# Projection of the last recurrent channel block before, instead of after, the MLP of the compressed values

## The chip, the cores and the metric

The kernel runs on one core of one Trainium2 chip. TensorE (PE) multiplies matrices into PSUM, VectorE (DVE) and ScalarE (ACT) read PSUM and work elementwise, GpSimd (POOL) works elementwise in SBUF, and the queue of SyncE (SP) issues nearly all DMAs. Each engine takes its own instructions in their order and waits on semaphores for the others. The metric is the device time of one execution in microseconds (us), the median of several runs.

## The reference, cut to what matters

One decoder block on x of shape (1024 tokens, 1024 channels). After an RMS norm one projection feeds two mixers, whose results are gated, added and projected out:

```
proj = rms_norm(x) @ w_in
y_a  = nsa_mixer(...)            # 8 heads in 2 groups: compressed, selected, sliding-window attention
y_b  = rglru_mixer(u_lru, ...)   # 512 channels
x + (sigmoid(gate_a) * (y_a * silu(g_nsa)) @ w_proj_a
     + sigmoid(gate_b) * (y_b * silu(g_lru)) @ w_proj_b) @ w_out
```

Two parts of it matter here. The recurrent mixer: a causal convolution of width 4 over `u`, two gates `r` and `i` from small block matrices, and a scan `h = a*h + b` over the 1024 tokens, with `a = exp(-8 r softplus(-lambda))`. And the compression of keys and of values: blocks of 32 tokens are flattened, 2048 inputs to 256 hidden units with SiLU, then 64 outputs, `silu(flat @ w1 + b1) @ w2`, once for keys (`kc`) and once for values (`vc`).

## The kernel before

All products of float32 values are made from a high and a low part: `mm3` (lines 170 to 173) issues three matmuls, high by high (L171), low by high (L172, the low part of the activations) and high by low (L173). A weight is loaded into `w_raw` (L177, two buffers), its high part is made by ACT (`w_hi`, L185, two buffers) and the low part by POOL or DVE (`w_lo`, L186). `hT_h` and `hT_l` (tiles `big_h`, `big_l`) hold the normed input, transposed.

After the norm the program has a stretch in which three kinds of work lie side by side on PE.

- `lru(n)` for the four channel blocks n of 128 channels. Its first part (call it A) projects `u` and the gate input: two chunks of 48 matmuls of 512 columns, then the copy to SBUF (L344), the convolution on DVE (L349, three times L352), the split (L355, L356) and a SiLU (L362, L363). Its second part (B) has four groups of three gate matmuls into `ps_t` (two buffers), each read by ACT as a sigmoid (L371); then ACT L377, L378 and L379 with table loads between them, DVE L380, L381, L383, L382 and the scan L384, POOL L372 and L385, and the store of the result to `yb` (L386).
- `compress()`: first the projections of keys and values, then for each of the two (j = 0 keys, j = 1 values) the copies of the blocks, the loads of w1 in eight pieces (L416, into buffers of `ph`, `pl` and `ev`), the MLP's first layer on PE (L422, 32 products in pairs of instructions), ACT L432, DVE L433 and L434, the second layer (L439) and, for the values, the split into `vcc` (L462, L463). The eighth piece of w1 goes into an `ev` buffer that the second piece has left, so its load is issued when the second piece's products are done.
- `qkv(0)`: queries, keys and values of the first head group, eight tiles of 128 tokens, 48 matmuls of 262 columns each; two of its four weight pieces are split into the tile `p_slc`, which compress() used before. Each tile's result is copied by ACT into an `ev` buffer (L519, L520; three buffers) and prepared by `prep`: ACT L552, DVE L554, POOL L193 and L194, DVE L557, POOL L558 and L559, ACT L562, L566 and L570, DVE L563 and L567, POOL L571, PE transposes L575 and L582 into `ps_t`, and their copies L577 and L586.

Queries, keys and the recurrent blocks' temporaries share nine tiles `t`. After this stretch comes the attention, in which the second group's projections and the merge's projections fill PE between the attention's own matmuls.

The order in which the pieces are written is set by a string; `0` to `3` stand for the next part of a recurrent block and `c` for the next part of `compress()`:

```
parts = {"0": lru(0), "1": lru(1), "2": lru(2), "3": lru(3), "c": compress()}
for k in ORD:
    next(parts[k])
```

With `ORD = "0c1c0c2c1c323"` the end reads: B of block 1, the MLP of the values, A of block 3, B of block 2, B of block 3. The framework's scheduler then puts the instructions of each engine into an order of its own by priorities (roughly the written order) and its own idea of when each could start, so a change of the string moves instructions on every engine for some way on.

Of the kernel before, what the change touches and what calls it, by code (L numbers as in the profile page):

```python
# [41 lines left out]
RW = 1  # L42
LE = 1
IE = 0
ORD = "0c1c0c2c1c323"
YE = 0
JE = 15
UE = 15
# [39 lines left out]
def _build(ctx, tc, A, out, dbg):  # L88
# [378 lines left out]
# [3 lines that stand above are left out]
# [662 lines left out]
```

## Time and profile before

| what | us |
|---|---|
| median of 3 runs (lowest, highest) | 893.48 (892.17, 894.21) |
| the profiled execution | 894.25 |
| its span, first to last instruction | 892.50 |
| PE busy in the span | 868.9 (97%) |
| DVE, ACT, POOL busy | 539.1, 449.8, 298.3 |

A row of the timeline gives the start, the length, the engine, line, operation, tile written <- tiles read, the shapes and the count, and in brackets how long the engine had been idle and what released it. A PE matmul's length is modelled to its end in the pipeline; the next matmul starts earlier, so starts are compared with starts. In a row of windows the busy time of each engine is followed by the number of its instructions, and the last three numbers are the granted clock of TensorE (1.00 is 2.4 GHz, 0.50 is 1.2 GHz), the busy share of the DMA engines and the GB/s.

### The profile page before, as it was taken

The page shows a single profiled execution, that of the slowest core. Times are in us where ns is not written, and L with a number is a line of the kernel's source. Part 1 is how long each engine was busy: PE and PEld are TensorE (multiplying, and loading weights), DVE is VectorE, ACT ScalarE, POOL GpSimd, SP SyncE. Part 2 cuts the span into 40 slices and gives each one's busy share as a digit, 9 for nine tenths or more (in the row PEclk, how much of TensorE's full clock was granted, in tenths as well). Part 3 has the DMA queues.
Part 4 walks back from the last instruction along what each step waited for, and adds up shares of the span by engine and source line. Part 5 has one row for each costly group of instructions (what it writes and reads, how often), then busy time and mean ns, then how long its engine had stood idle before and what let it go on. Part 6 is the DMA issues. An engine that isn't in the chain of part 4 may idle for free.

```text
span 892.5 us, 15853 instructions
## 1 busy us (share of the span) xinstructions
PE 868.9 (97%) x5670; PEld 778.3 (87%) x5670; DVE 539.1 (60%) x1629; ACT 449.8 (50%) x1168; POOL 298.3 (33%) x338
## 2 busy tenths in 40 slices
PE   5999999989999999999999999999999899999998
PEld 4778888889999999999999998999999887888887
DVE  4564547586423547566677857667777878892111
ACT  7322645845524647566556757566666563440000
POOL 4032243297512526244256644233334432000000
PEclk9999999999999999999999999999999999999999
DMA  9134420121312112211112241111114379971111
GB/s 352 58 98 117 158 84 26 63 71 51 131 45 84 59 67 72 66 60 65 53 62 77 75 140 53 33 70 55 33 45 127 128 245 341 362 257 71 71 72 47
DMA packets 45519, 92.49 MB, mean 104 GB/s; under 512 B 6896, under 2 KB 12704, under 8 KB 45440
## 3 DMA queue, kind: packets, MB, share of 16 engines
q1 hardware_dynamic: 44480, 88.33, 29.5%
q0 software_dynamic: 960, 3.15, 0.9%
q8 instruction: 44, 0.72, 0.3%
q14 instruction: 35, 0.29, 0.1%
HBM read 64.15 MB, written 25.21 MB: 100 GB/s over the span
## 4 chain that ended last, share of the span: by engine, by line
PE 82%; POOL 5%; ACT 4%; DMA 3%; DVE 3%; issue 1%; SPq 0%; POOLq 0%; ACTq 0%; DVEq 0%
PE ps_f L171 10%; PE ps_f L172 10%; PE ps_f L173 10%; PE ps_s L633 7%; PE ps_s L171 6%; PE ps_s L173 6%; PE ps_s L172 6%; PE ps_t L686 6%; PE ps_t L171 3%; PE ps_t L172 3%; PE ps_t L173 3%; PE ps_o L711 3%; PE ps_o L710 3%; DMA w_raw<-in_w_out 1%; PE ps_s L422 1%
## 5 line engine op out<-in xcount | busy, mean ns | idle before, releaser
L172 PE MATMUL ps_f<-big_l,w_hi 128*128 128x256 f32 (+1 forms) x712 | 204.8, 288 | 0.0
L171 PE MATMUL ps_f<-big_h,w_hi 128*128 128x256 f32 (+1 forms) x664 | 193.7, 292 | 1.0 <-ACT ev L852 0.9
L173 PE MATMUL ps_f<-big_h,w_lo 128*128 128x256 f32 (+1 forms) x664 | 189.3, 285 | 0.0
L172 PEld LDWEIGHTS ps_f<-big_l,w_hi 128*128 128x128 f32 x712 | 135.0, 190 | 2.3
L171 PEld LDWEIGHTS ps_f<-big_h,w_hi 128*128 128x128 f32 x664 | 125.2, 189 | 5.0 <-ACT ev L852 2.5
L173 PEld LDWEIGHTS ps_f<-big_h,w_lo 128*128 128x128 f32 x664 | 124.8, 188 | 1.8 <-POOL w_lo L186 0.3
L691 DVE TENSOR_TENSOR pl<-ps_t,ph 128x512 fp32r<-128x512 f32 x132 | 90.4, 687 | 47.1 <-ACT ph L690 45.7
L186 POOL TENSOR_TENSOR w_lo<-w_raw,w_hi 128x1024 fp32r<-128x1024 f32 x32 | 77.4, 2422 | 97.7 <-ACT w_hi L185 75.7
L690 ACT ACTIVATE ph<-ps_t 128x512 fp32r<-128x512 f32 x132 | 78.2, 600 | 49.5 <-PE ps_t L686 45.3
L671 POOL TENSOR_SCALAR p_slc<-p_slc,mx,bg 128x384 f32<-128x384 f32 (+7 forms) x88 | 68.6, 785 | 87.3 <-DVE mx L670 33.1
L667 ACT ACTIVATE p_slc<-ps_s,mx 128x256 f32<-128x256 f32 (+5 forms) x128 | 68.2, 541 | 23.4 <-DVE mx L665 16.6
L172 PE MATMUL ps_s<-big_l,w_hi 128*128 128x512 f32 x172 | 69.6, 405 | 0.0
L185 ACT ACTIVATE w_hi<-w_raw 128x1024 fp32r<-128x1024 f32 (+1 forms) x40 | 42.4, 1062 | 42.8 <-PE ps_f L172 17.3
L657 DVE TENSOR_REDUCE mx<-ps_s 128x1 f32<-128x256 f32 (+5 forms) x120 | 51.0, 437 | 10.5 <-PE ps_s L633 9.2
L710 PE MATMUL ps_o<-ph,t 128*128 128x512 f32 x132 | 55.5, 420 | 0.0
L171 PE MATMUL ps_s<-big_h,w_hi 128*128 128x512 f32 x136 | 54.1, 406 | 0.3 <-ACT big_h L246 0.3
L686 PE MATMUL ps_t<-ident_r,p_slc 128*128 128x128 f32 x336 | 54.0, 273 | 0.0
L173 PE MATMUL ps_s<-big_h,w_lo 128*128 128x512 f32 x136 | 54.0, 399 | 0.0
L662 DVE CUSTOM_DVE_ANT_0 ps_s<-ps_s,bias 128x256 f32<-128x256 f32 (+1 forms) x128 | 52.6, 417 | 1.6 <-PE ps_s L633 0.5
L633 PE MATMUL ps_s<-kTs,t 128*128 128x512 f32 (+4 forms) x224 | 52.9, 348 | 0.5 <-ACT pc L642 0.3
L711 PE MATMUL ps_o<-pl,t 128*128 128x512 f32 x132 | 53.2, 403 | 0.0
L671 POOL TENSOR_SCALAR p_win<-p_win,mx,bg 128x640 f32<-128x640 f32 (+1 forms) x40 | 35.0, 878 | 49.7 <-DVE mx L670 22.2
(368 smaller groups left out, 2182.2 us busy)
## 6 DMA issues: line engine op xcount, KB each, us to landing
w_raw<-in_w_in SPq DMA_DIRECT2D x30, 512.0 KB
t<-in_x SPq DMA_DIRECT2D x8, 512.0 KB
gb<-ev SPq DMA_DIRECT2D x16, 256.0 KB
ga<-ev SPq DMA_DIRECT2D x16, 256.0 KB
w_raw<-in_w_out SPq DMA_DIRECT2D x8, 512.0 KB
st<-mb SPq DMA_DIRECT2D x16, 256.0 KB
w_raw<-in_w_tok SPq DMA_DIRECT2D x6, 524.0 KB
ev<-in_cw SPq DMA_DIRECT2D x8, 256.0 KB
```

Of the source, the lines that this page charges most:

```text
L171: T.matmul(o, lh, rh, start=first, stop=False)
L172: T.matmul(o, lh, rl, start=False, stop=False)
L173: T.matmul(o, ll, rh, start=False, stop=last)
L186: (E or (V if tail else G)).tensor_tensor(out=lo, in0=raw, in1=f(hi), op=OP.subtract)
L633: T.matmul(s, qT[h][:, i * 128:(i + 1) * 128], rhs, start=(hl == 0), stop=(hl == 1))
L667: C.activation(p[:, h, k0:k1], sv, AF.Exp, bias=mx[:, 6:7], accum_out=mx[:, 7 + j:8 + j])
L671: G.tensor_scalar(out=p[:, h], in0=p[:, h], scalar1=mx[:, 9:10], scalar2=bg[:, g, i, 4 * (br + 1) + h:4 * (br + 1) + h + 1], op0=OP.mult, ...
L686: ins = T.transpose(pt[:, h * 128:(h + 1) * 128], p[h][:, c0:c0 + 128], ident)
L690: C.activation(ph, pt, AF.Copy)
L691: V.tensor_tensor(out=pl, in0=pt, in1=f(ph), op=OP.subtract)
L710: T.matmul(o, vf, pp[0], start=first, stop=False)
L711: T.matmul(o, vf, pp[1], start=False, stop=False)
```

## The change

One letter of the order string changes places with its neighbour: A of block 3 is written ahead of the MLP of the values.

```diff
-ORD = "0c1c0c2c1c323"
+ORD = "0c1c0c2c13c23"
```

No operation is added or removed. What the scheduler makes of it differs on every engine, from the last gates of block 1 to the first units of the attention; from there on the orders are the same again. On PE the 32 products of L422 move behind the 96 chunk matmuls of block 3 and stand there in one piece, directly ahead of qkv(0). Three places are shown.

On SP's queue, around the loads of the token weights (`w_raw<-in_w_tok`) and the eighth piece of w1 (`ev<-in_cw`), the difference is:

```order
 L498 DMA p_win<-in_w_tok 128x1048 x2
 L386 DMA yb<-t 128x1024
-L177 DMA w_raw<-in_w_tok 128x1048
+L177 DMA w_raw<-in_w_tok 128x1048 x3
+L386 DMA yb<-t 128x1024
 L416 DMA ev<-in_cw 128x512
 L177 DMA w_raw<-in_w_tok 128x1048
 L426 DMA t<-in_cw 128x128
-L386 DMA yb<-t 128x1024
-L177 DMA w_raw<-in_w_tok 128x1048 x2
```

The store of block 1's result (the second `yb` row) now stands ahead of the eighth piece of w1 and not behind it, and two more loads of token weights stand ahead of that piece.

On POOL, at the first tiles of `prep` (`ss_1355`, `sq_1353`, `ev_1349` belong to the first tile, `1446`, `1444`, `1440` to the second, `1537`, `1535`, `1531` to the third; `t_1203` is block 2's result), the order before was:

```order
L193 TENSOR_SCALAR ss_1355<-ss_1355 128x6
L194 TENSOR_TENSOR ss_1355<-ss_1355,nhalf_77 128x6
L385 TENSOR_TENSOR t_1203<-t_1203,kTs_427 128x1024
L558 TENSOR_TENSOR sq_1353<-sq_1353,small_73 128x256
L559 TENSOR_TENSOR sq_1353<-sq_1353,small_73 128x128
L571 TENSOR_TENSOR t_1271<-ev_1349,t_1271 128x64
L571 TENSOR_TENSOR t_1271<-ev_1440,t_1271 128x64
L571 TENSOR_TENSOR t_1272<-ev_1349,t_1272 128x64
L571 TENSOR_TENSOR t_1272<-ev_1440,t_1272 128x64
L193 TENSOR_SCALAR ss_1446<-ss_1446 128x6
```

and it is now, from block 2's L385 on:

```order
L385 TENSOR_TENSOR t_1203<-t_1203,kTs_427 128x1024
L558 TENSOR_TENSOR sq_1444<-sq_1444,small_73 128x256
L559 TENSOR_TENSOR sq_1444<-sq_1444,small_73 128x128
L193 TENSOR_SCALAR ss_1537<-ss_1537 128x6
L571 TENSOR_TENSOR t_1271<-ev_1349,t_1271 128x64
L571 TENSOR_TENSOR t_1271<-ev_1440,t_1271 128x64
L571 TENSOR_TENSOR t_1271<-ev_1531,t_1271 128x64
L194 TENSOR_TENSOR ss_1537<-ss_1537,nhalf_77 128x6
L571 TENSOR_TENSOR t_1272<-ev_1349,t_1272 128x64
```

The last reader of the first tile's `ev_1349` was the third L571 behind block 2's L385, straight after the first tile's own products; it now stands behind those of the second tile, the root L194 of the third and three more L571. The fourth tile's eviction (L519 into `ev_1622`) uses that buffer again.

On DVE the last block's chain (`t_1236`, `t_1235` belong to block 3) stood before in this order, from its first operation to its scan:

```order
L380 SCALAR_TENSOR_TENSOR t_1236<-t_1108,t_1236 128x1024
L381 SCALAR_TENSOR_TENSOR t_1235<-t_1108,t_1235 128x1024
L476 COPY bias_1247<-t_1248 128x1024
L554 TENSOR_REDUCE ss_1446<-sq_1444 128x6
L563 TENSOR_TENSOR st_1376<-sq_1353,st_1376 128x4x64
L383 TENSOR_TENSOR t_1176<-t_1176,t_1236 128x1024
L567 TENSOR_TENSOR st_1379<-sq_1353,st_1379 128x2x128
L476 COPY bias_1247<-t_1251 128x1024
L382 TENSOR_SCALAR t_1235<-t_1235 128x1024
L521 COPY bg_358<-ps_f_1451 128x12
L481 COPY cbias_357<-t_1254 128x512
L557 TENSOR_TENSOR sq_1444<-ev_1440,ss_1446 128x384
```

(one L554 and the scan L384 follow), and now the second tile's L557 stands ahead of it and the third tile's inside it:

```order
L557 TENSOR_TENSOR sq_1444<-ev_1440,ss_1446 128x384
L554 TENSOR_REDUCE ss_1537<-sq_1535 128x6
L380 SCALAR_TENSOR_TENSOR t_1236<-t_1051,t_1236 128x1024
L381 SCALAR_TENSOR_TENSOR t_1235<-t_1051,t_1235 128x1024
L476 COPY bias_1247<-t_1248 128x1024
L563 TENSOR_TENSOR st_1467<-sq_1444,st_1467 128x4x64
L567 TENSOR_TENSOR st_1470<-sq_1444,st_1470 128x2x128
L383 TENSOR_TENSOR t_1119<-t_1119,t_1236 128x1024
L476 COPY bias_1247<-t_1251 128x1024
L382 TENSOR_SCALAR t_1235<-t_1235 128x1024
L557 TENSOR_TENSOR sq_1535<-ev_1531,ss_1537 128x384
```

Behind these follow L577, L521, L554, L481 and the scan L384. Block 3's operations have fallen back by one tile of `prep`.

## Rows read from the trace of the kernel before

**Rows 1.** The page's head: span, and busy time of TensorE.

```profile
span 892.5 us, 15853 instructions
PE 868.9 (97%) x5670; PEld 778.3 (87%) x5670; DVE 539.1 (60%) x1629; ACT 449.8 (50%) x1168; POOL 298.3 (33%) x338
```

**Rows 2.** Windows of 5 us: length, then busy us of PE, PEld, DVE, ACT, POOL, then granted clock, DMA share, GB/s.

```profile
170.00:175.00 5.00, 3.27 (x26) 3.02 (x26) 2.40 (x3) 4.96 (x6) 0.00 (x0) 1.00 0.00 0
...
185.00:190.00 5.00, 3.21 (x28) 3.00 (x26) 5.00 (x8) 1.99 (x8) 4.76 (x6) 1.00 0.46 141
...
195.00:200.00 5.00, 3.12 (x27) 2.91 (x26) 4.22 (x8) 2.25 (x8) 4.83 (x5) 1.00 0.02 7
```

**Rows 3.** Timeline of PE: the four late starts between 170 and 205 us, and the matmul ahead of the second.

```profile
174.62 0.50 PE L171 MATMUL ps_t<-t,bias 128*128 128x512 f32 x1 [1.73 <-ACT t L371]
...
187.69 0.28 PE L173 MATMUL ps_s<-p_slc,big_l 128*128 128x262 f32 x1
189.76 0.54 PE L575 MATMUL ps_t<-ident_r,st 128*128 128x128 f32 x4 [1.79 <-DVE st L563]
...
199.12 0.54 PE L575 MATMUL ps_t<-ident_r,st 128*128 128x128 f32 x4 [1.89 <-DVE t L577]
...
203.73 0.54 PE L582 MATMUL ps_t<-ident_r,st 128*128 128x128 f32 x4 [0.24 <-DVE t L586]
```

**Rows 4.** Timeline of PE: the first and the fourth product of L422 for the values, the first and the 43rd of a run of chunk matmuls without a break, the first of a run of 262 columns, and the last matmul of the last gate group.

```profile
126.65 0.38 PE L422 MATMUL ps_s<-p_slc,ph 128*128 128x128 f32 x2
...
127.32 0.39 PE L422 MATMUL ps_f<-p_slc,ph 128*128 128x128 f32 x2
...
148.96 0.50 PE L173 MATMUL ps_s<-big_h,w_lo 128*128 128x512 f32 x1
...
158.78 0.40 PE L173 MATMUL ps_s<-big_h,w_lo 128*128 128x512 f32 x1
...
176.13 0.40 PE L173 MATMUL ps_t<-t,bias 128*128 128x512 f32 x1
...
178.31 0.28 PE L171 MATMUL ps_s<-w_hi,big_h 128*128 128x262 f32 x1
```

**Rows 5.** Timeline of SP's queue: the eighth piece of w1, the store of block 1, and two token weights behind it (256, 512 and 524 KB, the row of two loads is the span from the first to the second).

```profile
129.33 0.33 SPq L416 DMA_DIRECT2D ev<-in_cw  x1
...
154.04 0.33 SPq L386 DMA_DIRECT2D yb<-t  x1
154.47 8.30 SPq L177 DMA_DIRECT2D w_raw<-in_w_tok  x2
```

**Rows 6.** Windows of 2 us around the store: the last two numbers are the DMA share and GB/s.

```profile
154.00:156.00 2.00, 2.00 (x10) 1.62 (x9) 1.97 (x4) 0.87 (x2) 0.02 (x1) 1.00 0.60 229
156.00:158.00 2.00, 2.00 (x10) 1.65 (x9) 1.93 (x3) 0.00 (x0) 0.00 (x0) 1.00 0.92 293
```

**Rows 7.** Timeline of ACT: block 1's L379; then block 3's last two sigmoids, its L377 and its L379.

```profile
138.88 1.06 ACT L379 ACTIVATE t<-t 128x1024 f32<-128x1024 f32 x1
...
176.15 1.25 ACT L371 ACTIVATE t<-ps_t,small 128x512 f32<-128x512 f32 x2
177.44 1.15 ACT L377 ACTIVATE t<-t,m4sp 128x1024 f32<-128x1024 f32 x1
...
182.91 1.06 ACT L379 ACTIVATE t<-t 128x1024 f32<-128x1024 f32 x1
```

**Rows 8.** Timeline of DVE: block 1's L382 and block 3's; a tile's L557 beside POOL's L385 and one alone; block 3's L380 and its scan.

```profile
145.07 2.95 DVE L382 TENSOR_SCALAR t<-t 128x1024 f32<-128x1024 f32 x1
...
182.41 2.75 DVE L557 TENSOR_TENSOR sq<-ev,ss 128x384 f32<-128x384 f32 x1 [1.17 <-POOL ss L194]
...
185.16 1.21 DVE L380 SCALAR_TENSOR_TENSOR t<-t 128x1024 f32<-128x1024 f32 x1
...
191.96 0.80 DVE L382 TENSOR_SCALAR t<-t 128x1024 f32<-128x1024 f32 x1
...
195.04 2.58 DVE L384 TENSOR_TENSOR_SCAN t<-t 128x1024 f32<-128x1024 f32 x1
...
210.05 0.56 DVE L557 TENSOR_TENSOR sq<-ev,ss 128x384 f32<-128x384 f32 x1 [1.01 <-POOL ss L194]
```

**Rows 9.** Timeline of POOL: block 1's L385, L194 of the first tile (beside a scan on DVE) and of a later one, block 3's L385.

```profile
150.70 3.32 POOL L385 TENSOR_TENSOR t<-t,kTs 128x1024 f32<-128x1024 f32 x1 [3.24 <-DVE t L384]
...
179.06 3.31 POOL L194 TENSOR_TENSOR ss<-ss,nhalf 128x6 f32<-128x6 f32 x1
...
198.29 1.32 POOL L194 TENSOR_TENSOR ss<-ss,nhalf 128x6 f32<-128x6 f32 x1
199.58 2.39 POOL L385 TENSOR_TENSOR t<-t,kTs 128x1024 f32<-128x1024 f32 x1
```

**Rows 10.** Windows of 1 us around another late start of PE, with the granted clock as the third number from the end.

```profile
692.00:693.00 1.00, 0.00 (x0) 0.00 (x0) 1.00 (x1) 1.00 (x4) 1.00 (x2) 1.00 0.00 0
...
694.00:695.00 1.00, 1.00 (x5) 1.00 (x6) 1.00 (x4) 0.66 (x3) 0.86 (x1) 0.51 0.73 176
...
697.00:698.00 1.00, 1.00 (x9) 1.00 (x8) 0.97 (x2) 0.00 (x0) 0.00 (x0) 0.78 0.89 289
```

**Rows 11.** Timeline of PE: that start.

```profile
693.95 0.54 PE L171 MATMUL ps_f<-big_l,w_hi 128*128 128x256 f32 x1 [1.97 <-DVE ev L899]
```

## The prediction

> **What bounds the kernel now.** First the page's head: PE is busy 868.9 of 892.5 us [rows 1], so only PE's late starts and its share of other engines' waits can be won or lost. Then the windows: of the stretch that the change touches, three windows of 5 us show PE at 3.27, 3.21 and 3.12 us [rows 2]. The timeline of PE names the causes: at 174.62 it waits for a gate sigmoid on ACT (the buffers of `ps_t` are both in use), at 189.76 for the first tile's split on DVE (L563), at 199.12 and 203.73 for copies out of `ps_t` (L577, L586) that stand behind block 3's scan on DVE or its L385 on POOL [rows 3]. A PE row is modelled 0.28 us long, but the next 262-column matmul starts (187.69 - 178.31) / 77 = 0.122 us later [rows 3, 4], so each late start lost 0.16 us more than its idle time. The four lost 1.73 + 1.79 + 1.89 + 0.24 + 4 x 0.16 = 6.3 us.
>
> The change adds and removes no work. It moves the MLP's 32 products to a place behind block 3's chunks and moves block 3's gates and vector chain later. From the first units of the attention on, all orders are equal, and PE is what bounds there; so the whole difference is PE's late starts after the change less 6.3 us.
>
> **Part 1: the MLP's weights.** A product of L422 takes (127.32 - 126.65) / 3 = 0.223 us, a 512-column matmul (158.78 - 148.96) / 42 = 0.234 us [rows 4]. Before, L422 began at 126.65. Now 96 chunk and 9 gate matmuls come first: 126.65 + 105 x 0.234 = 151.2. The eighth piece of w1 is wanted 28 products later, at 157.5. Its load is issued when the second piece is used up, which would be at 153.0, but on SP it now stands behind the store of block 1. When is that? Block 1's fourth gate group stood behind 19 products and 9 matmuls (6.3 us past 126.65, its own included) and now ends after 42 matmuls (9.8 us): 3.5 us later. So L379 ends not at 139.94 but at 143.4 [rows 7]. From there to the end of L385 it was 14.1 us (154.02 [rows 9]). L382 took 2.95 us there beside POOL's split of the token weight and 0.80 alone [rows 8]; that split is now elsewhere, so I take 14.1 - 2.2 = 11.9 and let the other operations that enter and leave cancel. The store is issued at 155.3, the piece 0.43 us after it as the next DMA was before [rows 5]. Before, 512 + 524 KB were in transit for 0.60 x 2 + 0.92 x 2 = 3.0 us of full load within 4.0 us of the store's issue [rows 5, 6]; 512 + 256 KB are three quarters, so 2.3 us and the same 0.9 of delay: landed at 158.5. PE waits **1.0 us**. Bounds: 0, if the store is out by 153; 2.5, if DVE's three long convolution steps all go ahead of POOL's L385 instead of one.
>
> The split of the values' second token weight (`p_slc`) cannot begin before L422 ends, and PE wants it at the earliest 30 + 26 matmuls of 0.122 us and 12 others later, some 8 us; two splits on ACT, one on DVE and one on POOL of at most the length of an L385 [rows 9] are an estimated 5. I cost it at nothing; if DVE's and POOL's splits block each other it is up to 1 us.
>
> **Part 2: the gate wait.** Block 3's third gate group still needs a buffer that ACT frees only after block 2's L377 to L379 with their table loads (6.5 us from 177.44 to 183.97 for the same row of operations in block 3 [rows 7]), one more load and one sigmoid. From the end of L422 PE has 127 x 0.122 + 18 x 0.234 = 19.7 us of work, with the second layer's eight short matmuls some 20.4, up to it. ACT gets block 2's last sigmoid at 13.5 us and adds 6.5 + 1.9, less about half a us for evictions that now stand elsewhere: 21.5. PE waits **1.2 us** (before: 1.89); bounds 0 and 2.5.
>
> **Part 3: from block 3's last gate to the second tile's transposes.** This is the term that decides. Before: the last gate group was issued by 176.36 [rows 4] and L582 began at 203.73 [rows 3], 27.4 us, in these steps: ACT to the end of L379, 183.97, 7.6; DVE's L380 begins 1.2 later at 185.16; to the end of the scan, 197.62, 12.5; to the end of L385 on POOL, 201.97, 4.35; to L582, 1.76 [rows 3, 7, 8, 9]. PE had 23.0 us of work for that time and lost the rest.
>
> Now PE has less to put in: 169 matmuls of 0.122 us and three groups of transposes (0.54 modelled [rows 3], less the same 0.16 of overlap: 0.38), 21.7 us. And the chain carries more. L380 stands behind the second tile's L557, which meets block 2's L385 on POOL: 2.75 us beside such an L385, 0.56 alone [rows 8]. So I put 2.7 for the second step in place of 1.2. The scan stands behind the third tile's L557, which waits for a root (L194) that POOL reaches only after the second tile's products and three L571. I leave that step at its 12.5, the row it is nearest to. Sum 7.6 + 2.7 + 12.5 + 4.35 + 1.76 = 28.9, and PE waits 28.9 - 21.7 = **7.2 us** in that stretch. Most of it will show at one place: the fourth tile's eviction into `ev_1622` must wait for the first tile's last L571, and PE needs the PSUM buffer which that eviction frees.
>
> Bounds of the chain: if no operation of DVE and POOL holds another up, the third step is about 10 us, the fourth 2.4 and the second 1.2: 23.0. If they take turns all the way (an L194 takes 3.31 us beside a scan and 1.32 otherwise [rows 9]), the third step is 14.2 and the fourth 4.7: 31.0.
>
> These meetings are the place for a rule. In the rows, L382, L557 and L194 are long only while the other of DVE and POOL has a long operation [rows 8, 9]. The Trainium skill, "SBUF — State Buffer", section "SBUF: two separate sides", says that VectorE and GpSimd share a pair of ports as an exclusive lock held for a whole instruction, for VectorE instructions with two SBUF inputs or in a 2-port mode. By it the chain lies between 27 and 31; without it at 23, and the change would gain.
>
> **Sum.** 1.0 + 1.2 + 7.2 - 6.3 = +3.1 us. The profiled execution took 894.25 (span 892.50), 0.77 above the median of 893.48; from it 897.35, against the median 896.6. I forecast **896.6**.
>
> **Rivals.**
> - *The same chain, and weights in time.* Part 3 stays 27.4 because POOL is less loaded when the first tile comes (block 3's L372 is no longer ahead of it), and part 1 costs nothing: 0 + 1.2 + 5.7 - 6.3 = +0.6, so 894.1. For it: the same operations in nearly the same company. Against: the order on DVE puts two tiles' L557 into the chain, not one.
> - *Faster.* The first tile's transposes no longer wait (the 189.76 start is gone in any case, since its operations now lie ahead of block 3's), and block 3's chain finds DVE and POOL free: 23.0. Then 1.0 + 1.2 + 1.3 - 6.3 = -2.8, so 890.7. It decides from a chain under 25.8, where the sum is zero. For it: POOL was idle most of 155 to 175 and could do the first tile then. Against: block 3's L380 to scan took 12.5 us before with fewer operations ahead [rows 8].
> - *The clock falls.* Some 4 of the 7.2 us would be one idle piece. After a late start of 1.97 us at 693.95 [rows 11] the granted clock was 0.51 and came back between 697 and 698 [rows 10]: 3.4 us at 1.2 GHz, 1.6 lost. After the waits of 1.73 to 1.89 it stayed at 1.00 [rows 2, 3]. If it falls once: +4.7, 898.2. The Trainium skill, "TensorE: Matmul & The Clock Gate", section "Part 1: The HAM clock gate (the "warmup" mystery)", says that an array idle of late gets half of the pulses; by that page this rival would be the likelier case, by the three waits here it need not come.
>
> **Chances.** Forecast (chain 27.5 to 31 and the clock kept, 895.3 to 898.6): 0.45. Clock falls: 0.15. Same: 0.25. Faster: 0.15. A measurement of this kernel tells from no change about 0.2%, 1.8 us. Slower by more: 0.45 + 0.15 less a little of the forecast's lower edge, 0.58. Within: 0.27. Faster by more: 0.15. The range of 8 in 10 reaches down into the faster case and over the clock's: 892.0 to 900.0.
>
> **What would show it.** Right: one wait of about 1 us among the last products of L422, for the DMA of the eighth piece, with the store of `yb` directly ahead on SP; a gate wait near 1.2 us; no wait for the first L563; a wait of several us inside qkv(0) for an eviction (L519) whose releaser is POOL's L571; block 3's scan ending 5 us or more later than 197.6; windows of 1.00 clock. Wrong: L422 without a wait (part 1 falls); block 3's L385 ending before 204 (part 3 falls, and the time is at or under 893); a clock of 0.5 behind the long wait (the clock's case); or a difference that first shows beyond 245 us, where the orders are equal, which no term here has.

## The result and the profile after

The changed kernel took 898.62 us (median of 4 runs, 897.44 to 898.87) against 892.92 for the kernel before (4 runs): ratio 1.0054, 95% interval 1.0041 to 1.0068, so 3.7 to 6.1 us slower (the two medians by themselves are 5.7 apart). Forecast were 896.6 and a loss of 3.1; the time lies within the range, nearest to the figure of the rival with the fallen clock (898.2). The profiled execution took 898.44. One execution each of two later runs took 1717.9 and 947.7 us and is left out of their ratios.

The page's head of the changed kernel (PE's row as in [rows 1]) shows the same work in a span that is 4.1 us longer:

```profile
span 896.6 us, 15855 instructions
PE 868.8 (97%) x5670; PEld 778.3 (87%) x5670; DVE 536.6 (60%) x1629; ACT 449.6 (50%) x1168; POOL 297.1 (33%) x338
```

PE's late starts, from the timeline of PE (compare [rows 3]). Five, where the kernel before had four and a small one:

```profile
158.91 1.16 PE L422 MATMUL ps_s<-p_slc,ev 128*128 128x128 f32 x8 [1.23 <-DMA ev<-in_cw]
...
181.95 0.50 PE L171 MATMUL ps_t<-t,bias 128*128 128x512 f32 x1 [1.35 <-ACT t L371]
...
202.12 0.39 PE L171 MATMUL ps_s<-w_hi,big_h 128*128 128x262 f32 x1 [3.65 <-ACT ev L519]
...
214.37 0.54 PE L575 MATMUL ps_t<-ident_r,st 128*128 128x128 f32 x4 [0.72 <-DVE t L586]
...
234.31 0.68 PE L633 MATMUL ps_s<-t 128*128 128x384 f32 x3 [2.24 <-ACT t L586]
```

The first three are where the forecast had them and near its sizes. The fourth is the end of block 3's chain, seen one tile later than the forecast looked. The last, at the attention's first scores, stood nowhere in it.

Windows of 1 us behind the third start (the granted clock is the third number from the end):

```profile
202.00:203.00 1.00, 0.88 (x7) 0.88 (x8) 0.50 (x4) 0.97 (x5) 0.52 (x2) 0.98 0.03 8
203.00:204.00 1.00, 1.00 (x6) 1.00 (x6) 1.00 (x3) 0.90 (x5) 0.88 (x3) 0.50 0.00 0
...
206.00:207.00 1.00, 1.00 (x8) 1.00 (x8) 0.40 (x3) 0.30 (x1) 1.00 (x2) 0.81 0.00 0
207.00:208.00 1.00, 1.00 (x12) 1.00 (x10) 0.68 (x2) 0.71 (x4) 0.83 (x3) 1.00 0.00 0
```

TensorE's clock fell to 1.2 GHz for some 3.4 us, which is 0.02 + 3 x 0.50 + 0.19 = 1.7 us of full speed.

The account: after, 1.23 + 1.35 + 3.65 + 0.72 + 2.24 = 9.2 of waits, 5 x 0.16 of start-up and 1.7 of clock, 11.7. Before, the 6.3 of the prediction and another 0.45 at 231.76 us (a wait of 0.29 and its start-up, which the prediction left out). The difference is 4.95. A landmark behind it, the start of the first L686 (1314 matmuls stand ahead of it in both kernels), went from 240.13 to 244.85, 4.7 later, and a late start for ACT's L852 from 690.06 to 695.08, 5.0 later. From the timeline of PE before:

```profile
231.76 0.39 PE L171 MATMUL ps_s<-w_hi,big_h 128*128 128x262 f32 x1 [0.29 <-ACT p_win L667]
...
240.13 0.38 PE L686 MATMUL ps_t<-ident_r,p_win 128*128 128x128 f32 x2
```

and after:

```profile
244.85 0.38 PE L686 MATMUL ps_t<-ident_r,p_win 128*128 128x128 f32 x2
```

That the profiled spans differ by 4.1 only comes mostly from the clock: behind [rows 11] the kernel before lost it [rows 10], and this execution, with the same wait, did not.

```profile
698.98 0.38 PE L171 MATMUL ps_f<-big_l,w_hi 128*128 128x256 f32 x1 [1.98 <-DVE ev L899]
```

Block 3's chain (compare [rows 7 to 9]). The timeline of ACT: block 3's L379, the fourth tile's eviction, and the first copy behind L385.

```profile
191.59 1.06 ACT L379 ACTIVATE t<-t 128x1024 f32<-128x1024 f32 x1
...
201.68 0.39 ACT L519 ACTIVATE ev<-ps_s 128x262 f32<-128x262 f32 x1 [3.33 <-POOL t L571]
...
212.32 0.27 ACT L586 CAST kTs<-ps_t 128x128 fp32r<-128x128 f32 x1 [1.61 <-POOL t L385]
```

The timeline of DVE: the second tile's L557 beside block 2's L385, block 3's L380 and its scan.

```profile
191.35 2.74 DVE L557 TENSOR_TENSOR sq<-ev,ss 128x384 f32<-128x384 f32 x1 [1.39 <-POOL ss L194]
...
194.48 1.52 DVE L380 SCALAR_TENSOR_TENSOR t<-t 128x1024 f32<-128x1024 f32 x1
...
203.73 2.41 DVE L384 TENSOR_TENSOR_SCAN t<-t 128x1024 f32<-128x1024 f32 x1
```

The timeline of POOL: the third tile's root L194, the L571 behind it (the first of the three frees the eviction's buffer), an L558 beside the scan, and block 3's L385.

```profile
199.06 2.37 POOL L194 TENSOR_TENSOR ss<-ss,nhalf 128x6 f32<-128x6 f32 x1
201.33 1.19 POOL L571 TENSOR_TENSOR t<-ev,t 128x64 fp32r<-128x64 f32 x3
...
203.96 2.71 POOL L558 TENSOR_TENSOR sq<-sq,small 128x256 f32<-128x256 f32 x1
...
209.90 2.39 POOL L385 TENSOR_TENSOR t<-t,kTs 128x1024 f32<-128x1024 f32 x1
```

The last gate group was issued by 184.92 (its last matmul starts at 184.69), and L575 began at 214.37: 29.45 us, forecast 28.9.

### The profile page after: what moved, and what is told of

Same layout as the page of the kernel before. It is cut to its first block, busy times and chain, and to the rows that moved or that the text cites. A ratio compares the mean times of both kernels' runs of the same rounds, so it can differ in the third digit from the quotient of the medians.

```text
span 896.6 us, 15855 instructions
## 1 busy us (share of the span) xinstructions
PE 868.8 (97%) x5670; PEld 778.3 (87%) x5670; DVE 536.6 (60%) x1629; ACT 449.6 (50%) x1168; POOL 297.1 (33%) x338
## 4 chain that ended last, share of the span: by engine, by line
PE 79%; DVE 5%; DMA 5%; POOL 5%; ACT 4%; issue 2%; SPq 0%; ACTq 0%; POOLq 0%; DVEq 0%
PE ps_f L171 10%; PE ps_f L172 9%; PE ps_f L173 9%; PE ps_s L633 7%; PE ps_s L171 6%; PE ps_s L173 6%; PE ps_s L172 6%; PE ps_t L686 6%; PE ps_t L171 4%; PE ps_t L172 4%; PE ps_t L173 4%; PE ps_o L711 3%; PE ps_o L710 3%; DMA w_raw<-in_w_out 1%; POOL ss L194 1%
## 5 line engine op out<-in xcount | busy, mean ns | idle before, releaser
L172 PE MATMUL ps_f<-big_l,w_hi 128*128 128x256 f32 (+1 forms) x720 | 207.3, 288 | 0.0
L171 PE MATMUL ps_f<-big_h,w_hi 128*128 128x256 f32 (+1 forms) x672 | 196.8, 293 | 1.0 <-ACT ev L852 0.9
L173 PE MATMUL ps_f<-big_h,w_lo 128*128 128x256 f32 (+1 forms) x672 | 192.4, 286 | 0.0
L172 PE MATMUL ps_s<-big_l,w_hi 128*128 128x512 f32 x164 | 66.5, 405 | 0.0
L686 PE MATMUL ps_t<-ident_r,p_slc 128*128 128x128 f32 x336 | 54.2, 273 | 0.1
L633 PE MATMUL ps_s<-kTs,t 128*128 128x512 f32 (+4 forms) x224 | 52.9, 348 | 0.4 <-ACT pc L642 0.3
L171 PE MATMUL ps_s<-big_h,w_hi 128*128 128x512 f32 x128 | 50.8, 406 | 0.4 <-ACT big_h L246 0.4
L173 PE MATMUL ps_s<-big_h,w_lo 128*128 128x512 f32 x128 | 50.8, 399 | 0.0
```

The source lines that it names most:

```text
L171: T.matmul(o, lh, rh, start=first, stop=False)
L172: T.matmul(o, lh, rl, start=False, stop=False)
L173: T.matmul(o, ll, rh, start=False, stop=last)
L633: T.matmul(s, qT[h][:, i * 128:(i + 1) * 128], rhs, start=(hl == 0), stop=(hl == 1))
L686: ins = T.transpose(pt[:, h * 128:(h + 1) * 128], p[h][:, c0:c0 + 128], ident)
```

## The experiments

The theory behind them: block 3's chain across ACT, DVE and POOL sets the third tile's L575, whatever PE does inside it; the wait at L633 is a loss of its own. Rivals: the eviction or the clock is what costs, or each wait hides the next. Each result is the ratio to the kernel before, timed in the same rounds, with its interval; 0.001 is 0.9 us. The changed kernel itself was timed again only in the rounds of the first four runs. Where a later run is set against it or against a run of other rounds, two ratios are compared, and a difference under about 1.7 us is not clear of the noise.

**The changed kernel once more.**

> The changed kernel as it is, timed in the same rounds as the three that follow. Expected 898.6 us, 5.7 over the kernel before (bounds 4.5 and 6.8), with the same five late starts of PE: 1.2 at L422, 1.4 at L171 of the gates, 3.7 at the fourth tile's first matmul, 0.7 at L575 and 2.2 at L633.

Measured: 897.66 us, 1.0051 (1.0036 to 1.0066). Its profile has the same five waits (1.29, 1.35, 3.65, 0.69, 2.24). Six executions fell into two groups, 897.2 to 897.7 and 899.3 to 899.5.

**The eighth weight piece in an idle buffer.**

```diff
-t = te() if q % 2 else ...
+t = te2("ep") if (j, q) == (1, 7) else te() if q % 2 else ...
```

> The eighth piece of the values' first weight goes into a buffer that is idle until the attention (ep) instead of the ev buffer that its second piece leaves. Theory: the 1.23 us that PE waits for this transfer, with 0.16 of start-up, are lost for good, because ACT's gates, the token weight and block 3's chain all follow PE; so the wait goes and the time falls by 1.4 us, to 897.2. Rival: the next wait, for block 2's gate on ACT (1.35 us now), takes its place and becomes 2.6; then the time stays at 898.6.

Measured: 898.71, 1.0056 (1.0042 to 1.0071): no gain, against the theory. No engine's order changed but for that load. The wait for the DMA is gone, and two others stand behind it on PE, neither of them the gate that the rival named (it kept its 1.35). The timeline of PE:

```profile
158.94 0.39 PE L171 MATMUL ps_s<-w_hi,big_h 128*128 128x262 f32 x1 [0.52 <-DVE kTs L363]
...
163.37 0.76 PE L439 MATMUL ps_t<-t 128*64 128x64 f32 x8 [0.90 <-DVE t L434]
```

From the first L422 (150.74) to L439 it is 12.63 us; in the changed kernel 163.68 - 151.27 = 12.41. DVE was nearly as late as the weight: it comes out of 5.9 us of convolution steps beside POOL's L385, and L434 then took 2.46 us beside POOL's split, 0.49 in the changed kernel.

**The split off POOL.**

```diff
-QE = 0x77
+QE = 0xF7
```

(Each bit of `QE` gives one split to POOL, 0, or to DVE, 1.)

> The fourth split of the second half's token weight (L186, 2.41 us on POOL at 231.07) goes to DVE. Theory: PE's unforeseen wait of 2.24 us at L633 comes from DVE's L563 at 231.28, which took 2.48 us beside that split and 0.43 us elsewhere, with the copies (L586) that L633 wants queued behind it; without the split on POOL, L563 takes 0.43 to 0.55, the wait falls under 0.4 and the time falls by 1.8 to 2.4 us, to 896.5. Rival: the copies are late because their whole chain of tiles is late (first tile's keys wait for block 3's L385 until 212.29); then the wait stays at 2 us or moves, and the time stays within 0.6 us of 898.6.

Measured: 896.63, 1.0032 (1.0020 to 1.0045), 1.7 us under the changed kernel of the same rounds by the ratios (the medians are 1.0 apart); the intervals overlap a little, but the profile shows the step itself. The wait at L633 is gone. The timeline of DVE in the changed kernel:

```profile
231.28 2.48 DVE L563 TENSOR_TENSOR st<-sq,st 128x256 fp32r<-128x256 f32 x1
233.68 0.28 DVE L586 CAST kTs<-ps_t 128x128 fp32r<-128x128 f32 x1
```

and with the split on DVE:

```profile
232.04 0.42 DVE L563 TENSOR_TENSOR st<-sq,st 128x256 fp32r<-128x256 f32 x1
232.38 0.29 DVE L586 CAST kTs<-ps_t 128x128 fp32r<-128x128 f32 x1
```

The copy that the scores wanted stood behind an L563 that POOL's split (231.07, 2.41 us) held up for 2 us. The Trainium skill, "SBUF — State Buffer", section "SBUF: two separate sides", has the two engines take turns for whole instructions; L563 has two SBUF inputs, and these rows agree: it ended at 233.76, 0.28 us behind the split.

This profile also shows what the clock is worth inside the chain. It was down for twice as long, in windows of 2 us:

```profile
200.00:202.00 2.00, 0.00 (x0) 0.00 (x0) 1.92 (x5) 0.33 (x2) 2.00 (x3) 0.61 0.00 0
202.00:204.00 2.00, 1.89 (x8) 1.89 (x9) 1.50 (x6) 1.85 (x8) 1.40 (x5) 0.50 0.02 4
204.00:206.00 2.00, 2.00 (x12) 2.00 (x11) 2.00 (x1) 0.00 (x0) 2.00 (x1) 0.50 0.02 4
206.00:208.00 2.00, 2.00 (x13) 2.00 (x13) 1.08 (x5) 1.02 (x4) 1.83 (x4) 0.68 0.00 0
```

and the third tile's L575 still began 214.35 - 186.39 = 27.96 us behind the first tile's, against 27.97 in the changed kernel, now without its wait of 0.72. Of the longer fall PE worked through some 5.2 us (from 202.11 to 207.3), so it cost 2.6 of full speed in place of 1.7, and the 0.9 between them is the wait and its start-up: the clock took the place of the wait. In the run with the idle buffer PE worked through 6.0 us of a fall of the same length, and there this start came at 28.25, without a wait; a fall beyond what the chain leaves free does cost time.

**A buffer for the first tile.**

```diff
-e = te()
+e = te2("eo") if tb == NT - 1 and not g else te()
...
-(V.tensor_copy if BE else C.copy)(bg[:, g, tb], ...)
+(V.tensor_copy if g or tb != 4 else C.copy)(bg[:, g, tb], ...)
```

> The first tile's projection gets a buffer of its own (eo, idle until the attention) and the fourth tile's small copy L521 goes from DVE to ACT, so that the fourth tile's eviction waits neither for the first tile's last L571 on POOL nor for DVE. Theory: the 3.65 us and the clock that fell behind them (half speed for 3.4 us, 1.7 lost) lie inside block 3's chain, which ends with L385 at 212.3 and the copies at 214.3 whatever PE does; so the wait at that place goes, 3 to 5.5 us of it come back at the second and third tile's transposes (L575), L385 still ends at 212 to 213, and the time stays at 898.6, less at most 0.8. Rival: the eviction is what costs; then the time falls by 4 to 5.5 us, to about 894.

Measured: 898.47, 1.0053 (1.0038 to 1.0068): no change. The 3.65 us at the eviction are gone and came back at the second tile, by the timeline of PE:

```profile
205.02 0.75 PE L575 MATMUL ps_t<-ident_r,st 128*128 128x128 f32 x4 [3.28 <-DVE t L577]
...
212.99 0.54 PE L575 MATMUL ps_t<-ident_r,st 128*128 128x128 f32 x4 [0.55 <-DVE t L586]
```

The third tile's L575 is 27.23 behind the first's (185.76), 0.7 earlier than in the changed kernel. The largest wait of the profile was worth this 0.7 at most and nothing that the times show, as the theory had it.

**Block 3's L385 on DVE.**

```diff
-YE = 0
+YE = 8
```

(Each bit of `YE` gives the L385 of one block to POOL, 0, or to DVE, 1.)

> In the changed kernel, block 3's last product L385 goes from POOL (2.39 us, begun 3.8 us after the scan's end) to DVE, where it stands behind the scan and four short operations. Theory: block 3's chain sets the third tile's L575 (28.0 us behind the first tile's L575 in three profiles, whether the clock fell for 3.4 or for 6.8 us before it). L385 on DVE would end at some 209.5 in place of 212.3 and the copies 2 us later, so PE reaches that L575 without a wait and is then bound by its own work and the slow clock in front of it: the gain is the 0.7 us of wait and 0.16 of start-up where the clock falls for 3.4 us, to 897.0, and less where it falls for longer; at least 0 and at most 1.5. Rival (the chain is not what sets the place): no change, 897.7 to 898.6, with the wait at L575 still there.

Measured: 898.33, 1.0053 (1.0037 to 1.0068): nothing gained, the lower end of the theory's range. The trace is that of one more execution:

> The run with block 3's L385 on DVE once more, for a profile alone. Expected: the wait of 0.7 us at the third tile's L575 gone, the wait of 3.65 at the fourth tile's eviction and the fallen clock behind it still there, and the third tile's L575 within 0.9 us of 28.0 behind the first tile's.

Measured: 899.08 in one execution. The wait at the third tile's L575 is gone and that start is 27.1 behind the first tile's, which looks like the gain that was expected. It is none: nine matmuls that stood ahead of it in the changed kernel stand behind it here. With the same number of matmuls behind the first tile's L575, the 182nd, PE is at 28.05 here and at 27.97 there. L385 took 1.21 us on DVE, at 207.97, and the clock was down for 6.8 us, through 5.9 of which PE worked. The 2.24 at L633 turned into a start of L575 at 234.18, 1.69 late for a copy L577, which stood behind an L567 of 2.46 us (0.4 to 0.5 elsewhere), beside the split on POOL again, and the clock fell behind it a second time. What the shorter way of L385 would be worth at a kept clock is not shown.

**A shorter chain.** The edits of the buffer and

```diff
-YE = 0
+YE = 12
...
-V.tensor_copy(bias[:, q * 4:(q + 1) * 4], raw[:, :, ::-1])
+C.copy(bias[:, q * 4:(q + 1) * 4], raw[:, :, ::-1])
```

> In the changed kernel the first tile has a buffer of its own, the fourth tile's L521 is on ACT (as in the run with that buffer), and block 3's chain is made shorter: L385 of blocks 2 and 3 on DVE in place of POOL, and the two copies of the bias (L476, 0.68 us each, within the chain) on ACT in place of DVE. Theory: the chain is the bound; it loses some 2.2 us of DVE's L557 held up by block 2's L385, 1.4 of the copies and 2.5 of the way to L385, gains 1.2 for block 2's L385, and so the third tile's L575 comes 24 to 25 us behind the first tile's in place of 28.0: 3 to 4 us less, 894.4 us, with the wait of 2.2 us at L633 still there. Rival (PE's slow clock or the buffers set it): the gain is under 1 us, 897.5.

Measured: 896.44, 1.0033 (1.0022 to 1.0044), 1.6 us under the changed kernel; the two intervals overlap. The third tile's L575 moved to 212.18 - 186.79 = 25.4 behind the first's, without a wait, near the theory's 24 to 25. But here too the edits moved it in PE's order, 18 matmuls forward. The 182nd matmul behind the first tile's L575 started at 27.46, against 27.97, so PE gained 0.5 us up to this place and not 2.6. The scan ended only 0.9 us earlier (18.9 behind the first tile's L575, 19.7 in the changed kernel), since DVE now waited for POOL (1.21 us for an L557) where the copies had been, and PE waited 4.12 us for the copy L577 behind that scan, as its timeline has it:

```profile
206.33 0.54 PE L575 MATMUL ps_t<-ident_r,st 128*128 128x128 f32 x4 [4.12 <-DVE t L577]
...
233.08 0.54 PE L582 MATMUL ps_t<-ident_r,st 128*128 128x128 f32 x4 [0.47 <-DVE t L586]
```

The second row is what is left of the wait of 2.24 at L633, which the theory had staying. From the first tile's L575 to the first L686, 417 matmuls in both, it is 56.0 us here and 58.45 in the changed kernel. Of these 2.4 us only 0.5 lie before the 182nd matmul, so the 3 to 4 us that the theory expected of the chain did not come.

**The control: the split in the kernel before.**

> The control for the split: the kernel before with the fourth split of the second half's token weight on DVE in place of POOL, as in the run on the changed kernel. Theory: in the kernel before no copy for L633 stands behind that split, so it gains nothing: within 0.6 us of the kernel before (893.3). Rival (the split on POOL costs both kernels the same, and the changed kernel lost nothing by it): 1.8 to 2.4 us faster, 891.

Measured: 893.99, 0.9999 (0.9989 to 1.0010). The split costs the kernel before nothing that these times show; the wait at L633 belongs to the changed order, in which the late tiles of `prep` meet it.

**Both.** The shorter chain and the split:

> The shortened chain and the split on DVE together, in the changed kernel. Theory: both losses are real and apart, so their gains add: 3.5 + 1.8 = 5.3 us, 892.6, level with the kernel before (893.3). Rival (one takes the other's place): no better than the better of the two alone, 894.5 or more.

Measured: 895.08, 1.0017 (1.0006 to 1.0028), 3.1 us under the changed kernel, near the sum of the two gains as measured (1.6 and 1.7). That they are apart, as the theory has it, is not shown by this: over the 417 matmuls from the first tile's L575 to the first L686 the profiles have 58.45 us in the changed kernel, 55.95 with the split, 56.0 with the shorter chain and 55.3 with both, 2.5, 2.4 and 3.2 less. The wait at L633 is in both gains, and 0.5 us of the third comes from the place of the third tile. The theory's 5.3 took 3.5 for the shorter chain.

**The first tile's copies on ACT**, on top of both:

```diff
-(V.tensor_copy if h % 2 else C.copy)(qT[h]...
+(V.tensor_copy if h % 2 and (g or tb < NT - 1) else C.copy)(qT[h]...
```

> The changed kernel with the shortened chain and the split on DVE, and besides the first tile's four copies L577 all on ACT (two of them stood on DVE, the last one behind block 3's scan). Theory: with the chain shortened, the 4.2 us that PE waits at the second tile's L575 are the scan itself, since the copy behind it frees the PSUM buffer; off DVE the copy waits only for the loads of cbias and L481, ahead of the scan, so the wait falls to 1.5 to 2.5 us and the time by 1.5 to 2.5, to 893. Rival (the later copies L586 behind L385 set the third tile anyway): no change against the run before, 895.1.

Measured: 897.14, 1.0039 (1.0025 to 1.0053), 2 us slower than without. A miss. The timeline of ACT:

```profile
204.11 0.42 ACT L566 ACTIVATE st<-sq 128x256 fp32r<-128x256 f32 x1 [1.98 <-POOL sq L559]
204.43 0.41 ACT L577 CAST t<-ps_t 128x128 fp32r<-128x128 f32 x2
```

and of PE:

```profile
204.90 0.75 PE L575 MATMUL ps_t<-ident_r,st 128*128 128x128 f32 x4 [5.83 <-ACT t L577]
```

On ACT the copies stand behind two conversions that wait for POOL, whose L559 took 2.43 us beside DVE's scan (0.46 elsewhere). PE's order had moved L575 ahead, so the wait grew from 4.19 to 5.83, and the clock was down for 6.8 us.

**The same edits in the kernel before**, without and with the copies on ACT:

> The kernel before with the edits of the short chain and of the split (first tile's own buffer, the fourth tile's L521 on ACT, L385 of blocks 2 and 3 on DVE, the bias copies on ACT, the split on DVE). Theory: its own late starts at L577 and L586 (1.89 and 0.24) come from the same chain and go, the one at the gates (1.73) stays, so it gains 1.5 us, 891.6 (bounds 890 and 893.5), and the changed kernel with the same edits (895.1) stays behind it by some 3 us: the order of the change, not a side effect of one assignment, is what costs. Rival (the edits suit the changed order only): no gain, 893.1 or more.

> The kernel before with all of these edits and the first tile's L577 on ACT as well. Theory: as the run before it, and at most 0.5 us better, since there the copies stand less in the way: 891.3, bounds 889.5 and 893.5. It is the version that should beat both kernels.

Measured: 892.15, 0.9978 (0.9967 to 0.9990), and 891.35, 0.9973 (0.9960 to 0.9986). Both beat both kernels, by 2.0 and 2.4 us against the kernel before. The gain is of the size expected and lies elsewhere: the wait of 1.89 for a copy L577 is still 1.64 in the first of the two, and it is the wait for the first tile's L563 that went from 1.79 to 0.67, with the small ones at L582 and at 231.76 gone. With the same edits the changed order stays (1.0017 - 0.9978) x 893 = 3.5 us behind: most of its loss goes with the order and is not cured by them.

## Why the prediction was right, and where it was not

- *What bounds.* Right: PE's busy time is the same to 0.1 us, and its late starts with the clock account for 4.95 of the 4.7 to 5.0 at the landmarks.
- *Part 1.* The mechanism was right to the row: the store at 155.29 (155.3), the piece 0.42 behind it (0.43), 1.23 us of wait (1.0). As a term it was wrong: it did not ask what would be late next, and DVE was nearly as late as the weight, and taking the wait away gained nothing.
- *Part 2.* 1.35 for 1.2 (its own terms give 13.5 + 6.5 + 1.9 - 0.5 - 20.4 = 1.0); no wait for the first L563, as forecast.
- *Part 3.* Step by step, forecast and measured: to the end of L379 7.6 and 7.7; to L380 2.7 and 1.8; to the scan's end 12.5 and 11.7; to the end of L385 4.35 and 6.15; to the start on PE 1.76 and 2.1. Sum 28.9 and 29.45, which is luck in part: two steps were 0.8 to 0.9 too long and that to the end of L385 1.8 too short. The named meeting of L557 and block 2's L385 came (2.74 us), and the eviction waited for the L571 named. What PE lost in it is 3.65 + 0.72 + 2 x 0.16 + 1.7 = 6.4 against 7.2, because PE could still put in the second tile's four transposes and nine matmuls (1.4 us) before the place that the chain really held.
- *The clock rival.* The clock fell as it said, and its price was wrong. It added 1.6 to a chain that already set the time; clocks down for 3.4 and for 6.8 us ended at the same L575, so inside the chain the fall cost nothing, as far as the chain left room (up to 2.6 us). That the result is near this rival's 898.2 is an accident of the sum.
- *The step that failed* is the sentence that "from the first units of the attention on, all orders are equal", so that nothing is lost there. The first scores were the first reader of the late tiles, and 2.24 + 0.16 us were lost at it, shown by the split's run and its control. The order itself is not equal there: before, the first L633 stands on PE behind the transposes L575 of six tiles, and now behind those of five. With the start-up the three parts came to 1.4 + 1.5 + 6.4 = 9.3 for 9.4, their errors cancelling. With the scores and the 0.45 left out of the before's starts the forecast's +3.1 becomes 3.1 + 2.4 - 0.45 = 5.05.
- *Same chain* and *faster* fell: they wanted a chain of 27.4 or under 25.8.

Open: whether the chain is all that holds the third tile's place. That it does is read from its rows and from the runs in which the eviction's wait and the clock changed and the place stayed; the run that was to shorten it moved the scan by 0.9 us and the place by 0.5, and no run took it away. Open too are whether Part 1 and 2 would count if the chain were shorter still, and how far the two groups of times are the clock alone. The mean granted clock of the six executions of the repeated kernel, 0.996 to 0.998 in the lower group and 0.994 and 0.996 in the upper, does not part them.

## What to carry to other kernels

Price the chain that holds a place and the work that lies beside it, not the wait that is largest: a wait inside a longer chain, and a fallen clock too, only move when they are taken away. A landmark measures time lost only where the same work stands ahead of it; where an edit changes an engine's order, count its instructions first. Where an order changes, follow the late pieces to their first reader behind the stretch, and see what stands ahead of that reader's input on each in-order engine. Ask of each wait that a forecast counts what would have been late without it.

## What was not expected of the hardware

Over a wide range the length of a late start of PE does not by itself decide whether the clock falls. Between 126 and 705 us of the 13 profiles read here, all nine waits of 3.28 us and more were followed by 1.2 GHz. Of 26 between 1.64 and 2.24 us nine were: the same wait of 1.97 to 1.99 us for L899 in 6 of 13 profiles, one of 2.14 for L633 in the run with the idle buffer (of four there), one of 1.69 in the profile with L385 on DVE, and one of 1.73 in the control, where the same wait in the kernel before [rows 3] left the clock at 1.00. The prediction set three short waits of one profile against the clock's fall, where its own wait was to be longer than all of them. And the clock stayed down for about 3.4 us or for about 6.8, behind waits of the same 3.65 us. The Trainium skill, "TensorE: Matmul & The Clock Gate", section "Part 1: The HAM clock gate (the "warmup" mystery)", has the gate close on an array that has lately been idle; the long waits agree, and of the short ones a third; what parts these is not shown here.
